# A transfer of later stages' norm weights from GpSimd's queue at the start, and the lambda weights computed in the second pair of chunks

## The chip, the cores and the metric

The kernel runs on one core of a Trainium2 chip. The metric is the device time of one execution in microseconds (us); each run gives one time. The engines are named as in the profile: PE (TensorE's matmuls) and PEld (its weight loads), DVE (VectorE), ACT (ScalarE), POOL (GpSimd), and SP (SyncE, which issues most of the DMAs). A "q" behind a name (SPq) means the engine's instruction queue.

## What is computed

Two layers of a residual trunk over 256 tokens with 2048 columns, all in float32. Each layer has a mixer with two groups of eight heads (stick-breaking attention, and differential attention with a learned lambda) and a SwiGLU stage of width 5632. Cut to the places that matter here:

```python
def reference(x, ...):
    for l in range(DEPTH):                       # 2 layers
        h = rms_norm(x, pre_mix_norm[l])
        m = hybrid_mixer(h, l, ...)
        x = x + rms_norm(m, post_mix_norm[l])
        h = rms_norm(x, pre_ffn_norm[l])
        f = swiglu(h, w_gate[l], w_up[l], w_down[l])
        x = x + rms_norm(f, post_ffn_norm[l])

def hybrid_mixer(h, layer, w_in, w_o, ...):
    proj = h @ w_in                              # 2048 x 6144, q k v of both groups
    ...
    lam = (jnp.exp(jnp.sum(lq1 * lk1)) - jnp.exp(jnp.sum(lq2 * lk2)) + lam_init)
    o_d = differential_attention(q1, q2, k1, k2, v_d, lam)     # softmax1 - lam * softmax2
    o_d = rms_norm(o_d, diff_subln) * (1.0 - lam_init)
    return concat(o_sb, o_d) @ w_o
```

lambda depends on four vectors of 64 numbers for each layer, and on nothing else.

## The kernel before

**Precision by splitting.** Each float32 operand is split into a rounded part hi (made by ACT, line 286) and the rest lo (made by DVE, line 289), and each product is three matmuls: hi with hi (line 1017), hi with lo (1018), lo with hi (1019). All weights are read once from HBM, in one stream of tiles of 128x1024 (512 KB, named raw, GU, G, T or V) whose order `weight_order` fixes. `fetch` issues the loads on SP's queue, `feed` makes hi and lo, four tiles ahead of the product that needs them. There are four raw buffers and six each of hi and lo: a load waits until DVE has split the tile that had its buffer, and a split waits until PE has used up the tile three pairs of rows before.

**The input projection.** 12 chunks of 512 output columns are computed in six pairs (`PAIRS`: first 6 and 8, the rotary q and k of the differential group; then 10 and 7; and so on). For each pair a loop runs over the eight pairs of rows kp. For most kp there are eight products for the two chunks and the two halves of the tokens (`eight_in`, four ticks). From the second pair on, kp 4 and 5 use seven products in place of eight (`seven_in`, `seven_products`). For these, `mixed_weights` (lines 258 to 274) builds sums of weight blocks: DVE adds (264), ACT and DVE split (259, 260), DVE subtracts (267) and adds (268), and the sums are split into Th and Tl (259, 260). Their products go to the banks p and q (p_in, q_in in the profile). After the last seven-product step `shared_part` combines them on DVE (lines 1055 to 1058) into w.

**The opening.** The first pair of layer 0 runs in `opening`, which loads x by columns (xr) and the first weights in small pieces. Beside it `first_stats` loads x by rows (x0) for the norm's sums, and at its last step calls `late_constants`: the rest of the gains (columns 32 to 96: the norm weights of the ffn stage, of layer 1 and of both attention outputs), the rope table, the four lambda vectors broadcast to 128 partitions, some constant matrices made by POOL, and the whole arithmetic of lambda (lines 399 to 413), which ends in `lamsign`. At the start of the kernel POOL also makes the identity (`make_identity`, two instructions listed as masks.py:197 and masks.py:199); a cast of it to bf16 (line 393) runs on DVE in the opening, between the splits.

**After a pair.** `settle` evacuates the banks (tok, line 913, on ACT). For chunks 6 and 8 POOL rotates tok (lines 786 to 789, with the rope table). `flip` transposes them (qkT_ps on PE, qT and kT on ACT, line 932). `diff_weights` then makes the softmax weights and multiplies by `lamsign` (line 749): for the first time at 99.63 us.

**What sets the order.** The engines run their own instruction lists in order. The list is made by a scheduler from the program's order and estimated times. Generators started with `start` are advanced by `tick`, which the product loops call: a value that a generator yields is the number of ticks until its next step. `tc.issue_after(...)` keeps an instruction behind another one: `in_turn` behind the last weight load, `after_rests` behind the last split made on DVE, `not_ahead` behind a load some places earlier. DMAs on SP signal one of eight semaphores in rotation, so a load also waits for the transfer eight places ahead.

**Memory.** `late_constants` takes its temporary tiles from the tag t2 (four buffers, shared with the sums of the seven-product steps). `early_room` hands out four rooms of 128x1024 in rotation: first to the four x0 tiles, later to the outputs of the differential heads, then to the ffn stage.

Of the kernel before, what the change touches and what calls it, by code (L numbers as in the profile page):

```python
# [17 lines left out]
P = 128  # L18
D = 2048
S = 256  # L20
L = 2
# [36 lines left out]
def lambda_init(layer):  # L58
    return 0.8 - 0.6 * math.exp(-0.3 * layer)
# [94 lines left out]
def kernel(  # L154
# [153 lines left out]
    def in_turn():  # L308

        return tc.issue_after(loads[-1].ins)  # L310
# [67 lines left out]
    lamsign = const.tile([P, L, 4], F32, name="lamsign")  # L378

    def late_constants(pool):  # L380
        lams = pool.tile([P, 4, L * 64], F32, tag="t2", name="lams")
        negones = pool.tile([P, P], F32, tag="t2", name="negones")
        nc.sync.dma_start(gains[:, 32:96], gain_columns[:, 32:96])
        nc.sync.dma_start(rope_sb, rope.rearrange("(t p) c -> p t c", p=P))
        for i, v in enumerate((lambda_q1, lambda_k1, lambda_q2, lambda_k2)):
            nc.sync.dma_start(lams[:, i, :], v.rearrange("l d -> (l d)").partition_broadcast(P))
        nc.gpsimd.memset(negones, -1.0)
        nc.vector.tensor_copy(negone, negones)
        nc.gpsimd.affine_select(
            out=negones, in_=negones, compare_op=ALU.is_ge, fill=0.0, base=0, pattern=[[-1, P]], channel_multiplier=1  # L390
        )
        nc.vector.tensor_copy(negtri, negones)
        nc.vector.tensor_copy(ident16, ident)
        nc.gpsimd.memset(hidden, NEG)
        nc.gpsimd.affine_select(
            out=hidden, in_=hidden, compare_op=ALU.is_ge, fill=0.0, base=0, pattern=[[-1, P]], channel_multiplier=1
        )
        nc.gpsimd.memset(lamsign, 1.0)
        lprod = pool.tile([P, 2, L * 64], F32, tag="t2", name="lprod")
        lsum = pool.tile([P, 2, L], F32, tag="t2", name="lsum")  # L400
        for i in range(2):
            nc.vector.tensor_tensor(out=lprod[:, i, :], in0=lams[:, 2 * i, :], in1=lams[:, 2 * i + 1, :], op=ALU.mult)
            nc.vector.tensor_reduce(
                out=lsum[:, i, :], in_=lprod[:, i, :].rearrange("p (l d) -> p l d", l=L), axis=AX.X, op=ALU.add
            )
        nc.scalar.activation(lsum, lsum, AF.Exp)
        for l in range(L):
            c0 = 80 + l * NH
            nc.vector.tensor_scalar_mul(gains[:, c0 : c0 + NH], gains[:, c0 : c0 + NH], 1.0 - lambda_init(l))
            for q in range(2):  # L410
                col = lamsign[:, l, 2 * q + 1 : 2 * q + 2]
                nc.vector.tensor_tensor(out=col, in0=lsum[:, 1, l : l + 1], in1=lsum[:, 0, l : l + 1], op=ALU.subtract)
                nc.vector.tensor_scalar_add(col, col, -lambda_init(l))

    const.tile([P, LEVEL], F32, name="level")
    eps = const.tile([P, 1], F32, name="eps")
# [374 lines left out]
    def opening(pool, accs, xT, stats, sums_of, settle):  # L791

        xr = []

        def load():
            kp = len(xr)
            xr.append(pool.tile([P, 2, S], F32, tag="tok", name=f"xr{kp}"))
            nc.sync.dma_start(xr[kp], x_columns[:, 2 * kp : 2 * kp + 2, :])

        def split(k):  # L800
            g, src = gains[:, k : k + 1], xr[k // 2][:, k % 2, :]
            nc.scalar.activation(xT[k][:, 0, :], src, AF.Copy, scale=g)
            nc.vector.scalar_tensor_tensor(
                out=xT[k][:, 1, :], in0=src, scalar=g, in1=xT[k][:, 0, :].bitcast(F32), op0=ALU.mult, op1=ALU.subtract
            )

        load()
        both = []
        for i in range(2):
            both.append((  # L810
                wpool.tile([P, 2, CW], F32, tag="raw", bufs=4, name=f"raw{i}"),
                wpool.tile([P, 2, CW], F32R, tag="hi", bufs=6, name=f"hi{i}"),
                wpool.tile([P, 2, CW], F32R, tag="lo", bufs=6, name=f"lo{i}"),
            ))
            raws.append(both[i][0])
        for kk in range(2):
            for i in range(2):
                loads.append(nc.sync.dma_start(raws[i][:, kk, :], stream[i][:, kk, :]))
        load()
        fetch(4)  # L820
        for kk in range(2):
            split(kk)
            for raw, hi, lo in both:
                nc.scalar.activation(hi[:, kk, :], raw[:, kk, :], AF.Copy)
                nc.vector.tensor_tensor(out=lo[:, kk, :], in0=raw[:, kk, :], in1=hi[:, kk, :].bitcast(F32), op=ALU.subtract)
        for i in range(2):
            ready[i] = both[i][1:]
        fed[0] = 2
        for kp in range(KT // 2):
            if kp:  # L830
                split(2 * kp)
                split(2 * kp + 1)
            if kp + 2 < KT // 2:
                load()
                fetch(2 * kp + 6)
            for part in ((0,), (1,)) if kp == KT // 2 - 1 else (range(NT),):
                eight_in(accs, xT, 0, PAIRS[0], kp, part, kp == 0, kp == KT // 2 - 1, 0)
                if kp == KT // 2 - 1:
                    settle(part[0])
            if 3 <= kp < 7:  # L840
                next(stats)
            if kp >= 4 and kp - 4 < len(IN_SEVEN):
                sums_of(IN_SEVEN[kp - 4])
# [38 lines left out]
    def mixer_in(pool, l, rs, xT, mix, mixed):  # L882
# [7 lines left out]
        for n, cc in enumerate(PAIRS):  # L890
# [52 lines left out]

            if n == 0 and l == 0:
                opening(pool, banks, xT, first_stats(pool, rs), sums_of, settle)
            else:
                kps = IN_ORDER if n else tuple(range(KT // 2))
                extra = None
                burst[0] = clock[0] + 4 * kps.index(mine[0]) if mine and n else None
                for j, kp in enumerate(kps):  # L950
                    first, last = j == 0, j == len(kps) - 1
                    if n == 0 and 2 <= j < 2 + len(IN_SEVEN):
                        sums_of(IN_SEVEN[j - 2])
                    if n == 0 and 3 <= j < 7:
                        put_away(f"in{l}", j - 3)
                    if kp in mine:
                        if extra is None:
                            assert math.inf not in taken
                            extra = four_banks(True, [f"{q}_in{l}_{n}" for q in ("p1", "p6", "p7", "q5")])
                        seven_in(banks, extra, forms[kp], xT, l, cc, kp, kp == mine[0], kp == mine[-1])  # L960
                        if kp == mine[-1]:
                            burst[:] = None, clock[0] + SETTLE
                            w = pool.tile([P, 4, CW], F32, tag="gpost", bufs=1, name=f"w{l}_{n}")
                            with tc.high_priority(offset=URGENT):
                                shared_part(extra, [w[:, i, :] for i in range(4)])
                            if n + 1 < len(PAIRS) and IN_NOW[n + 1]:
                                burst[0] = clock[0] + 4 * (len(kps) - 1 - j) + 4 * IN_ORDER.index(IN_NOW[n + 1][0])
                            else:
                                pool.end_of_sums()
                                mix_pool[0] = pool  # L970
                        continue
                    if n == 0 and j < 2:
                        if j == 0:
                            for t in range(NT):
                                for kp in kps[:2]:
                                    eight_in(banks, xT, l, cc, kp, (t,), kp == kps[0], False)
                        continue
                    if first or last:
                        for t in range(NT):
                            eight_in(banks, xT, l, cc, kp, (t,), first, last)  # L980
                            if last:
                                settle(t)
                    else:
                        eight_in(banks, xT, l, cc, kp, range(NT), first, last)
                    if j == 0 and n == len(PAIRS) - 1:
                        xs[:] = [[late_room([P, D // 2], f"x{l}_{t}_{h}") for h in range(2)] for t in range(NT)]
                        with in_turn():
                            for t, h in ((0, 0), (0, 1), (1, 0), (1, 1)):
                                load_x(t, h, away[-1] if l else None)
# [387 lines left out]
```

## Time and profile before

| | |
|---|---|
| median of three runs | 2197.44 us (2195.82 to 2197.62) |
| profiled execution | 2197.66 us, span 2196.0 us |
| PE busy in the span | 2177.9 us (99%), 9991 matmuls |
| DVE, ACT, POOL busy | 1902.1 us (87%), 1370.5 us (62%), 138.6 us (6%) |
| HBM read, mean rate | 457.00 MB, 212 GB/s over the span |
| transfers issued by POOL | 110, the first at 417.23 us |
| gains, rope and the lambda loads issued by SP | at 34.16, 34.97, and 36.23 to 38.89 us |
| arithmetic of lambda on DVE | between 43.16 and 48.30 us |

How to read the lines below. A line of a timeline gives the start in us from the span's first instruction, the duration in us, the engine, the line of the kernel, the operation, the tile written and the tiles read, shapes, and how often. In brackets stands the idle time of the engine just before it, and what ended it. A line of the waits gives who waited for whom: us in total, times, longest. A line of the windows gives a stretch and its length, then for PE, PEld, DVE, ACT and POOL the busy time and the number of instructions, then the granted clock of TensorE as a share of full speed, the share of the DMA engines, and GB/s. Matmuls overlap, so the distance between starts tells PE's pace, not the duration of one.

### The profile page before, as it was taken

The numbers are of one execution on the slowest core, as the hardware profiler recorded it, in microseconds if no ns is written. First come the engines' busy times: TensorE is split into PE (matmuls) and PEld (weight loads), VectorE is DVE, ScalarE is ACT, GpSimd is POOL, SyncE is SP. The second block draws the span as 40 slices with busy tenths as digits, with TensorE's granted clock in tenths as the row PEclk, the third lists the DMA queues.
The fourth block names the chain that finished last, engine by engine and source line by source line (L and its number), as shares of the span: only waits on it lengthen the run. The fifth ranks groups of instructions, "written<-read, shape, count | busy, mean of one in ns | idle before, by whom it ended". The sixth has DMA issues, their size and how long they took to land.

```text
span 2196.0 us, 28541 instructions
## 1 busy us (share of the span) xinstructions
PE 2177.9 (99%) x9991; PEld 1790.8 (82%) x9991; DVE 1902.1 (87%) x2609; ACT 1370.5 (62%) x2052; POOL 138.6 (6%) x186
## 2 busy tenths in 40 slices
PE   9999999999999999999999999999999999999998
PEld 7788888788888888888878888888888888888886
DVE  7888658899999999989878886589999999999997
ACT  7566665756656656666665666657665566566664
POOL 1200000000001000000011000000000100100000
PEclk9999999999999999999999999999999999999999
DMA  9555555488687676767465455555867766767673
GB/s 308 200 170 173 192 182 172 155 279 256 196 266 243 197 251 203 244 214 262 151 251 173 160 179 189 192 170 190 276 216 244 258 216 224 241 212 234 206 266 98
DMA packets 138513, 467.28 MB, mean 213 GB/s; under 512 B 15872, under 2 KB 16640, under 8 KB 137856
## 3 DMA queue, kind: packets, MB, share of 16 engines
q1 hardware_dynamic: 122384, 436.59, 57.0%
q0 software_dynamic: 15840, 28.84, 7.5%
q8 instruction: 78, 1.28, 0.2%
q14 instruction: 67, 0.55, 0.1%
q10 hardware_dynamic: 144, 0.02, 0.0%
HBM read 457.00 MB, written 8.39 MB: 212 GB/s over the span
## 4 chain that ended last, share of the span: by engine, by line
PE 90%; DVE 4%; DMA 3%; ACT 2%; issue 1%; DVEq 0%; POOL 0%; ACTq 0%; POOLq 0%; SPq 0%
PE c L1018 9%; PE c L1019 9%; PE c L1017 9%; PE in L1017 6%; PE in L1019 6%; PE in L1018 6%; PE dn L1261 4%; PE dn L1259 4%; PE dn L1258 4%; PE p L1018 2%; PE p L1019 2%; PE p L1017 2%; PE o L528 2%; PE o L529 2%; PE o L530 2%; DMA raw<-in_weights_in_turn_dram 2%
## 5 line engine op out<-in xcount | busy, mean ns | idle before, releaser
L289 DVE TENSOR_TENSOR lo<-raw,hi 128x1024 fp32r<-128x1024 f32 x522 | 625.6, 1219 | 98.0 <-ACT hi L286 97.2
L286 ACT ACTIVATE hi<-raw 128x1024 fp32r<-128x1024 f32 x522 | 540.4, 1055 | 188.0 <-issue 51.8
L1017 PE MATMUL c<-hi,xF 128*128 128x512 f32 x834 | 328.0, 394 | 0.1
L1018 PE MATMUL c<-lo,xF 128*128 128x512 f32 x834 | 325.1, 390 | 0.7 <-DVE lo L289 0.7
L1019 PE MATMUL c<-hi,xF 128*128 128x512 f32 x834 | 324.8, 390 | 0.0
L238 POOL DMA_DIRECT2D T<-in_weights_in_turn_dram x110 | 95.9, 874 | 1684.5 <-DMA T<-in_weights_in_turn_dram 496.5
L1018 PEld LDWEIGHTS c<-lo,xF 128*128 128x128 f32 x834 | 156.7, 188 | 33.5 <-DVE lo L289 2.5
L1019 PEld LDWEIGHTS c<-hi,xF 128*128 128x128 f32 x834 | 156.5, 188 | 32.7
L1017 PEld LDWEIGHTS c<-hi,xF 128*128 128x128 f32 x834 | 156.7, 188 | 31.5 <-ACT xF L447 0.5
L1258 PE MATMUL dn<-hi,jh 128*128 128x512 f32 x432 | 168.3, 389 | 0.0
L1259 PE MATMUL dn<-lo,jh 128*128 128x512 f32 x432 | 168.1, 389 | 0.0
L289 DVE TENSOR_TENSOR lo<-G,hi 128x1024 fp32r<-128x1024 f32 x110 | 133.9, 1218 | 29.8 <-ACT hi L286 29.6
L259 ACT ACTIVATE hi<-T 128x1024 fp32r<-128x1024 f32 x110 | 115.5, 1050 | 45.6 <-PE c L1019 31.3
L259 ACT ACTIVATE Th<-G 128x1024 fp32r<-128x1024 f32 x110 | 116.1, 1055 | 37.9 <-DVE G L268 35.9
L260 DVE TENSOR_TENSOR Tl<-G,Th 128x1024 fp32r<-128x1024 f32 x110 | 133.9, 1217 | 5.3 <-ACT Th L259 5.3
L260 DVE TENSOR_TENSOR lo<-T,hi 128x1024 fp32r<-128x1024 f32 x110 | 133.9, 1217 | 4.3 <-ACT hi L259 4.0
L268 DVE TENSOR_TENSOR G<-G,T 128x1024 f32<-128x1024 f32 x110 | 134.2, 1220 | 2.1
L259 ACT ACTIVATE Th<-T 128x512 fp32r<-128x512 f32 x110 | 68.9, 627 | 104.6 <-DVE T L267 88.7
L1261 PE MATMUL dn<-hi,jl 128*128 128x512 f32 x432 | 132.9, 390 | 0.0
L1017 PE MATMUL in<-hi,xT 128*128 128x512 f32 x328 | 131.3, 401 | 0.0
L1017 PE MATMUL in<-hi,xI 128*128 128x512 f32 x328 | 131.1, 401 | 0.0
L1018 PE MATMUL in<-lo,xT 128*128 128x512 f32 x328 | 128.2, 391 | 0.4 <-DVE lo L289 0.4
(448 smaller groups left out, 4736.8 us busy)
## 6 DMA issues: line engine op xcount, KB each, us to landing
raw<-in_weights_in_turn_dram SPq DMA_DIRECT2D x522, 512.0 KB, 4.5
T<-in_weights_in_turn_dram SPq DMA_DIRECT2D x110, 512.0 KB, 6.3
G<-in_weights_in_turn_dram SPq DMA_DIRECT2D x110, 512.0 KB, 5.8
T<-in_weights_in_turn_dram POOLq DMA_DIRECT2D x110, 256.0 KB, 7.1
GU<-in_weights_in_turn_dram SPq DMA_DIRECT2D x32, 512.0 KB, 6.2
V<-in_weights_in_turn_dram SPq DMA_DIRECT2D x8, 512.0 KB, 4.1
away_ffn<-x SPq DMA_DIRECT2D x8, 512.0 KB, 8.4
xd<-away_ffn SPq DMA_DIRECT2D x8, 512.0 KB, 8.4
```

Of the source, the lines that this page charges most:

```text
L238: nc.gpsimd.dma_start(sums[i][:, 0, :], stream[i - 1][:, 0, :], accum_op=ALU.add)
L259: nc.scalar.activation(h, w, AF.Copy)
L260: nc.vector.tensor_tensor(out=l, in0=w, in1=h.bitcast(F32), op=ALU.subtract)
L268: nc.vector.tensor_tensor(out=g, in0=g, in1=t2.unsqueeze(1).to_broadcast([P, 2, CW]), op=ALU.add)
L286: nc.scalar.activation(hi, raw, AF.Copy)
L289: rest = nc.vector.tensor_tensor(out=lo, in0=raw, in1=hi.bitcast(F32), op=ALU.subtract)
L1017: nc.tensor.matmul(a, sh, hi, start=first, stop=False, skip_group_check=open_sums[0])
L1018: nc.tensor.matmul(a, sh, lo, start=False, stop=False, skip_group_check=open_sums[0])
L1019: nc.tensor.matmul(a, sl, hi, start=False, stop=last, skip_group_check=open_sums[0])
L1258: nc.tensor.matmul(accs[c, t], sh, hi[:, kk, :], start=first, stop=False, skip_group_check=open_sums[0])
L1259: nc.tensor.matmul(accs[c, t], sh, lo[:, kk, :], start=False, stop=False, skip_group_check=open_sums[0])
L1261: nc.tensor.matmul(accs[c, t], sl, hi[:, kk, :], start=False, stop=last, skip_group_check=open_sums[0])
```

## The change

The load of gains 32 to 96 is issued by POOL's queue and no longer by SP's. In the instruction list it stands near the start of POOL's queue, behind the memset of the identity and of eps, ahead of masks.py:199.

The lambda work leaves `late_constants`. A new generator `lambdas` is started when the opening's program has been written out, with its tiles in one early room. Its four loads are issued in turn with the weights; sixteen ticks later come the products, sums, the Exp and the scalings, with the first of them held behind the last split. In the instruction lists the four loads stand on SP behind the sixth weight load of the second pair; the arithmetic stands on DVE behind the two splits of kp 6 of the second pair and among the four instructions of `shared_part`, with the last steps around the two splits of kp 7. Exp stands on ACT between the first and the second copy into qT.

As the scheduler works from estimated times, some neighbours change places too. On DVE the copies negone and negtri stand earlier in the opening. For kp 4 and kp 5 of the second pair, one split of plain weights stands behind the subtraction (267) where it stood ahead of it, or behind the wide Tl where it stood ahead of it. On ACT the splits of the second pair's first four tiles stand partly ahead of the evacuations (tok) of the opening's banks; before, only the first one did. On PE, in both seven-product steps, the three products of p7 with the wide Th and Tl stand together, where other products stood between them. From about the third pair on the lists of all engines are the same.

```diff
--- before.py
+++ after.py
@@ -378,12 +378,9 @@
     lamsign = const.tile([P, L, 4], F32, name="lamsign")
 
     def late_constants(pool):
-        lams = pool.tile([P, 4, L * 64], F32, tag="t2", name="lams")
         negones = pool.tile([P, P], F32, tag="t2", name="negones")
-        nc.sync.dma_start(gains[:, 32:96], gain_columns[:, 32:96])
+        nc.gpsimd.dma_start(gains[:, 32:96], gain_columns[:, 32:96])
         nc.sync.dma_start(rope_sb, rope.rearrange("(t p) c -> p t c", p=P))
-        for i, v in enumerate((lambda_q1, lambda_k1, lambda_q2, lambda_k2)):
-            nc.sync.dma_start(lams[:, i, :], v.rearrange("l d -> (l d)").partition_broadcast(P))
         nc.gpsimd.memset(negones, -1.0)
         nc.vector.tensor_copy(negone, negones)
         nc.gpsimd.affine_select(
@@ -396,21 +393,33 @@
             out=hidden, in_=hidden, compare_op=ALU.is_ge, fill=0.0, base=0, pattern=[[-1, P]], channel_multiplier=1
         )
         nc.gpsimd.memset(lamsign, 1.0)
-        lprod = pool.tile([P, 2, L * 64], F32, tag="t2", name="lprod")
-        lsum = pool.tile([P, 2, L], F32, tag="t2", name="lsum")
+
+    def lambdas():
+
+        room = early_room([P, 2 * CW], "lams")
+        lams = room[:, 0 : 4 * L * 64].rearrange("p (i c) -> p i c", i=4)
+        lprod = room[:, 4 * L * 64 : 6 * L * 64].rearrange("p (i c) -> p i c", i=2)
+        lsum = room[:, 6 * L * 64 : 6 * L * 64 + 2 * L].rearrange("p (i l) -> p i l", i=2)
+        with in_turn():
+            for i, v in enumerate((lambda_q1, lambda_k1, lambda_q2, lambda_k2)):
+                nc.sync.dma_start(lams[:, i, :], v.rearrange("l d -> (l d)").partition_broadcast(P))
+        yield 16
         for i in range(2):
-            nc.vector.tensor_tensor(out=lprod[:, i, :], in0=lams[:, 2 * i, :], in1=lams[:, 2 * i + 1, :], op=ALU.mult)
+            with after_rests():
+                nc.vector.tensor_tensor(out=lprod[:, i, :], in0=lams[:, 2 * i, :], in1=lams[:, 2 * i + 1, :], op=ALU.mult)
             nc.vector.tensor_reduce(
                 out=lsum[:, i, :], in_=lprod[:, i, :].rearrange("p (l d) -> p l d", l=L), axis=AX.X, op=ALU.add
             )
         nc.scalar.activation(lsum, lsum, AF.Exp)
         for l in range(L):
             c0 = 80 + l * NH
-            nc.vector.tensor_scalar_mul(gains[:, c0 : c0 + NH], gains[:, c0 : c0 + NH], 1.0 - lambda_init(l))
+            with after_rests():
+                nc.vector.tensor_scalar_mul(gains[:, c0 : c0 + NH], gains[:, c0 : c0 + NH], 1.0 - lambda_init(l))
             for q in range(2):
                 col = lamsign[:, l, 2 * q + 1 : 2 * q + 2]
                 nc.vector.tensor_tensor(out=col, in0=lsum[:, 1, l : l + 1], in1=lsum[:, 0, l : l + 1], op=ALU.subtract)
                 nc.vector.tensor_scalar_add(col, col, -lambda_init(l))
+        yield
 
     const.tile([P, LEVEL], F32, name="level")
     eps = const.tile([P, 1], F32, name="eps")
@@ -943,6 +952,7 @@
 
             if n == 0 and l == 0:
                 opening(pool, banks, xT, first_stats(pool, rs), sums_of, settle)
+                start(lambdas())
             else:
                 kps = IN_ORDER if n else tuple(range(KT // 2))
                 extra = None
```

## The prediction, made before the changed kernel ran

> **What bounds the kernel.** I read the page's busy table first, then the waits of PE over the whole span, because in a kernel whose PE is busy 99% only those waits can be won back.
>
> ```profile
> PE 2177.9 (99%) x9991; PEld 1790.8 (82%) x9991; DVE 1902.1 (87%) x2609; ACT 1370.5 (62%) x2052; POOL 138.6 (6%) x186
> ```
> ```profile
> PE p L1018 <- DVE Tl L260: 1.8, 3, 0.9
> PE xT_ps L444 <- DVE xd L574: 1.4, 1, 1.4
> PE p L1017 <- ACT Th L259: 1.3, 1, 1.3
> PE p_in L1017 <- ACT Th L259: 1.3, 1, 1.3
> PE spare L367 <- DVE idle L364: 1.3, 1, 1.3
> PE c L1018 <- DVE lo L289: 0.7, 2, 0.4
> PE in L1018 <- DVE lo L289: 0.6, 2, 0.4
> ```
>
> All waits together are 8.4 us. The change touches the first pair of chunks and the second; there lie only the single p_in wait and, in part, the last row. The timeline of PE shows where p_in stands:
>
> ```profile
> 64.14 0.39 PE L1018 MATMUL q_in<-lo,shin 128*128 128x512 f32 x1
> 64.37 0.39 PE L1019 MATMUL q_in<-hi,slin 128*128 128x512 f32 x1
> 66.08 0.73 PE L1017 MATMUL p_in<-Th,shin 128*128 128x512 f32 x2 [1.31 <-ACT Th L259]
> ```
>
> Matmuls start 0.23 us apart (64.14 to 64.37), so the next was due at 64.60 and came at 66.08: 1.48 us lost. That is the prize. It is the first seven-product step (kp 4 of the second pair), which waits for the split Th of the mixed weights. Following Th backwards, in the chain of waits and on the timelines of ACT and DVE:
>
> ```profile
> 39.62 8.28 DMA raw<-in_weights_in_turn_dram
> ```
> ```profile
> 47.32 0.21 ACT L406 ACTIVATE lsum<-lsum 128x4 f32<-128x4 f32 x1 [4.92 <-DVE lsum L403]
> 47.98 1.06 ACT L286 ACTIVATE hi<-raw 128x1024 fp32r<-128x1024 f32 x1 [0.46 <-DMA raw<-in_weights_in_turn_dram]
> ```
> ```profile
> 51.98 1.26 ACT L913 ACTIVATE tok<-in,rs_in 128x512 f32<-128x512 f32 x2
> 53.12 1.07 ACT L286 ACTIVATE hi<-raw 128x1024 fp32r<-128x1024 f32 x1
> 54.07 1.07 ACT L286 ACTIVATE hi<-GU 128x1024 fp32r<-128x1024 f32 x1
> ```
> ```profile
> 55.41 1.34 DVE L289 TENSOR_TENSOR lo<-GU,hi 128x1024 fp32r<-128x1024 f32 x1
> 56.68 0.95 DVE L264 TENSOR_TENSOR GU<-GU,GU 128x512 f32<-128x512 f32 x1
> 58.75 1.37 DVE L260 TENSOR_TENSOR lo<-GU,hi 128x1024 fp32r<-128x1024 f32 x1 [1.13 <-ACT hi L259]
> 60.05 1.48 DVE L289 TENSOR_TENSOR lo<-raw,hi 128x1024 fp32r<-128x1024 f32 x1
> 61.45 0.81 DVE L267 TENSOR_TENSOR GU<-GU 128x512 f32<-128x512 f32 x1
> 62.19 1.34 DVE L289 TENSOR_TENSOR lo<-raw,hi 128x1024 fp32r<-128x1024 f32 x1
> 63.45 1.48 DVE L268 TENSOR_TENSOR GU<-GU,GU 128x1024 f32<-128x1024 f32 x1
> 64.86 0.68 DVE L260 TENSOR_TENSOR Tl<-GU,Th 128x512 fp32r<-128x512 f32 x1
> 65.46 1.21 DVE L289 TENSOR_TENSOR lo<-GU,hi 128x1024 fp32r<-128x1024 f32 x1
> 66.59 1.21 DVE L260 TENSOR_TENSOR Tl<-GU,Th 128x1024 fp32r<-128x1024 f32 x1
> ```
>
> The reader should see two idle stretches of ACT: 4.92 us for the lambda sums, 0.46 us for weights whose first load started only at 39.62, behind gains, rope and four lambda loads on SP, and landed 8.28 us later.
>
> **Part 1, five loads leave SP's queue ahead of the weights.** In the changed order SP has only rope between the last x load and the first raw of the second pair. That raw can go once its buffer is free. ACT stood idle from 42.40 (47.32 - 4.92), and it no longer has Exp ahead of the weights; the loads need to land only some 2.1 us sooner for two hi of 1.06 to be done before the tok copies, and five issues fewer ahead of them give that (an estimate; if not, it is the first rival). What is late next is PE: the two tok copies at 51.98 evacuate the last opening banks and stay where they are. In the changed order all four raw splits stand before them, so the hi that began at 53.12 is gone from there and hi<-GU begins at 53.12 instead of 54.07 and ends at 54.19. DVE then starts lo<-GU near 54.3, 1.1 us earlier than 55.41.
>
> **Part 2, the order on DVE.** The order in which the two programs issue differs here in one helpful place: the lo of 60.05 stands behind L267 instead of ahead of it. L267 therefore moves by 1.1 and by 1.4 more (60.05 to 61.45), to 58.95. One lo still lies between L267 and L268, as before, so L268 starts 2.0 later, at 60.95. Th came 1.52 after the start of L268 and took 1.06:
>
> ```profile
> 64.97 1.06 ACT L259 ACTIVATE Th<-GU 128x1024 fp32r<-128x1024 f32 x1 [1.09 <-DVE GU L268]
> ```
>
> So Th is ready near 63.5, 1.1 us before 64.60: the 1.48 us goes. But PE's order changes too. Before, PE ran the second use of Th and other products ahead of the first Tl of the wide half; now Th, Tl, Th stand together, so Tl<-GU 128x1024 is wanted at 64.83. On DVE it comes behind L268, the narrow Tl and one lo: 60.95 + 1.41 + 0.60 + 1.13 = 64.1 at the uncontended spacing, 64.25 if the lo is slowed like the one at 62.19; plus 1.21 gives 65.3 to 65.5. A new wait of 0.5 to 0.65 us takes part of the prize. I take 0.6; the ends are 0 (slowing gone) and 1.5 (nothing won).
>
> [...] Slowed and unslowed rows of the same POOL line:
>
> ```profile
> 50.59 0.31 POOL L787 TENSOR_TENSOR rb<-tok,rope_sb 128x64 f32<-128x64 f32 x1
> ```
> ```profile
> 60.40 1.31 POOL L787 TENSOR_TENSOR rb<-tok,rope_sb 128x64 f32<-128x64 f32 x1
> ```
>
> The rotations last at least until 61.7 and DVE's 128x1024 subtractions take 1.34 to 1.48 beside them against 1.21 alone. The rotations start from tok copies that PE paces, so I leave them in place. [...]
>
> **Part 3, the lambda work in the second pair.** Loads: four, behind the second GU load; their landing is not wanted until DVE comes to them near 78. Work on DVE, by the groups of that window:
>
> ```profile
> L402 DVE TENSOR_TENSOR lprod<-lams 128x128 f32<-128x128 f32 x2 | 0.6, 293 | 3.0 <-DMA lams<-in_lambda_k_dram 2.9
> L403 DVE TENSOR_REDUCE lsum<-lprod 128x2 f32<-128x128 f32 x2 | 0.6, 286 | 0.1
> ```
> ```profile
> L412 DVE TENSOR_TENSOR lamsign<-lsum 128x1 f32<-128x1 f32 x4 | 0.4, 154 | 0.3 <-ACT lsum L406 0.3
> ```
>
> With four more column steps and two scalings of gains, taken at the 154 ns of the last row, that is 0.6 + 0.6 + 10 x 0.154 = 2.7 us, set among the four combinations of the shared products, after all weights of kp 5, 3 and 6 are split. Queued behind them on DVE are the two splits of kp 7, then those of the next pair. The cover is DVE's own idle there:
>
> ```profile
> 86.81 2.36 DVE L289 TENSOR_TENSOR lo<-raw,hi 128x1024 fp32r<-128x1024 f32 x2 [3.24 <-ACT hi L286]
> ```
>
> 3.24 us hold 2.7, so I cost it at nothing; without that cover it would cost at most 2.7. Exp on ACT now waits for DVE between two copies of transposed q, with the second qT and two kT copies and the next hi queued behind it; it takes 0.21 and PE has the whole of kp 6 and 7 before it needs that hi. Nothing.
>
> **Part 4, the gains transfer on POOL.** It stands on POOL between two memsets and the select that finishes the identity. Its price there, from the only transfers that POOL issues before (the view of line 238), and the one reader that could be held:
>
> ```profile
> L238 POOL DMA_DIRECT2D T<-in_weights_in_turn_dram x110: 853/866/1218, 417.2 to 2132.5; - x110
> ```
> ```profile
> 1.22 0.29 POOL masks.py:199 TENSOR_SCALAR_AFFINE_SELECT ident<-ident 128x128 f32<-128x128 f32 x1
> ```
> ```profile
> 11.12 0.22 DVE L393 CAST ident<-ident 128x128 bf16<-128x128 f32 x1
> 12.18 2.52 DVE L289 TENSOR_TENSOR lo<-raw,hi 128x1024 fp32r<-128x1024 f32 x2 [0.83 <-ACT hi L286]
> ```
>
> 0.87 to 1.22 us moves the identity from 1.51 to 2.7 at worst; the cast reads it at 11.12. Hidden. Its 32 KB now fall among the first weights. The 512 KB load above took 8.28 us in a full queue; 32 KB at that pace are 0.5 us, at the other end is nothing. I charge 0.1, nearer to nothing, because the first loads are issued before it.
>
> **Sum.** -1.48 + 0.6 + 0.1 = -0.8 us. The profiled execution took 2197.66 (span 2196.0 and 1.7 around it), the median is 2197.44; I subtract from the median: 2196.6. From about 100 us on, the order on every engine is the same in both programs, so the rest shifts as a block. A change below 0.2% (4.4 us) is about what a measurement of this kernel can't tell from none.
>
> **Rivals.**
> - *The new wait takes all of it.* Tl's wait of 0.6 grows to 1.5 if the loads land as late as before (47.9): 2197.5. For: DVE's rows from 60.05 to 66.59 show no idle before them, so each slip is passed on. Against: ACT's 4.92 idle is gone. 18%.
> - *The clock.* Where PE was busy for only 3.78 of 6 us, the granted clock fell to 0.79:
>
> ```profile
> 430.00:436.00 6.00, 3.78 (x11) 2.67 (x11) 6.00 (x12) 4.53 (x5) 0.00 (x0) 0.79 0.00 0
> ```
>
> 0.21 of 6 us is 1.3 us. A shift by about 1 us can make it vanish (2195.3, with the whole prize 2194.6) or give another gap one of its own (2197.9, without the prize 2198.7). [...] 8%.
> - *The first POOL transfer is slow, and the kernel slower.* The identity's select is behind it, the cast behind that on DVE, and all weight splits behind the cast. It decides from 11.12 - 1.51 = 9.6 us, and with DVE's idle of 0.83 from 10.4; each us beyond it is a us of PE. A hold of 16 us gives 2197.4 - 0.8 + 5.6 = 2202.2. For: no POOL transfer before 417 is in the trace. Against: the longest of 110 is 1.22. [...] 10%, with which I count any other unforeseen wait of that size.
> - *Faster by over 4.4 us.* It would need more than half of all waits of PE, most of them in stages whose order doesn't change. 4%.
>
> **Numbers.** The forecast has 60%. The range 2194.0 to 2199.5 takes in the first two rivals with the clock either way and the spread of the three times (1.8 us); it leaves out the last two. Faster by over 0.2% 0.04, slower 0.10, within 0.86.
>
> **What would show it.** Right: the p_in wait on Th missing, one on Tl of 0.3 to 0.9 in its place near 65; first raw load of the second pair issued before 37; hi<-GU starting at 53.1; no new wait of PE between 75 and 100; POOL's transfer below 1.5 us and the cast near 11.1. Wrong: Th still waited for, DVE late on kp 7 near 88, or a gap of PE before 14.

## The result and the profile after

The changed kernel takes 2192.31 us (median of 14 runs, 2191.73 to 2193.77), the kernel before 2197.72 us in the same comparison (14 runs, 2195.46 to 2200.58). The ratio is 0.9975, with a 95% interval of 0.9968 to 0.9983: 5.4 us faster, where 0.8 was forecast. The profiled execution took 2192.54 us, with a span of 2190.8.

The busy table and the waits of PE, as for the kernel before (lines of the program from about 400 on now bear numbers higher by 9 or 10, so L1027, L1028 and L1029 are the three products):

```profile
PE 2175.4 (99%) x9991; PEld 1789.5 (82%) x9991; DVE 1901.4 (87%) x2609; ACT 1370.4 (63%) x2052; POOL 141.0 (6%) x187
```
```profile
PE xT_ps L453 <- DVE xd L583: 1.4, 1, 1.4
PE spare L367 <- DVE idle L364: 1.3, 1, 1.3
PE p L1028 <- DVE Tl L260: 0.8, 2, 0.5
PE c L1028 <- DVE lo L289: 0.7, 2, 0.4
PE in L1027 <- ACT xT L811: 0.6, 1, 0.6
PE in L1028 <- DVE lo L289: 0.5, 2, 0.3
PE p L1027 <- ACT Th L259: 0.4, 1, 0.4
```

The wait of p_in for Th (1.3) is gone, as forecast. But two more rows of the old table shrank that the forecast left alone: p on Tl from 1.8 to 0.8, p on Th from 1.3 to 0.4. These are banks of the ffn stage, not of the input projection. By the timelines the 1.3 on Th at 431.45 us and the 0.9 on Tl at 432.84 are gone altogether; the 0.4 on Th in this table is another wait, at 1560.62 us. (The new row of 0.6 on xT lies in the opening, at 6.88 us.) What happened there is seen when the same matmuls are put side by side. Timeline of PE, kernel before:

```profile
429.73 0.39 PE L1019 MATMUL q<-hi,sl 128*128 128x512 f32 x1
431.45 0.50 PE L1017 MATMUL p<-Th,sh 128*128 128x512 f32 x1 [1.33 <-ACT Th L259]
432.84 0.50 PE L1018 MATMUL p<-Tl,sh 128*128 128x512 f32 x1 [0.88 <-DVE Tl L260]
...
435.08 0.63 PE L1018 MATMUL c<-lo,sh 128*128 128x512 f32 x1
435.51 0.63 PE L1019 MATMUL c<-hi,sl 128*128 128x512 f32 x1
...
437.05 0.39 PE L1017 MATMUL p<-hi,xF 128*128 128x512 f32 x1
```

And the changed kernel:

```profile
428.47 0.39 PE L1029 MATMUL q<-hi,sl 128*128 128x512 f32 x1
428.70 0.39 PE L1027 MATMUL p<-Th,sh 128*128 128x512 f32 x1
428.93 0.39 PE L1028 MATMUL p<-Tl,sh 128*128 128x512 f32 x1
...
431.42 0.39 PE L1027 MATMUL p<-hi,xF 128*128 128x512 f32 x1
```

Up to q<-hi,sl the changed kernel is 1.26 us ahead (429.73 - 428.47), at p<-hi,xF it is 5.63 ahead (437.05 - 431.42). So 4.4 us of the gain lie in one place of some 8 us, the first seven-product step of the ffn stage of layer 0, some 340 us behind the last instruction that the change moves. Two things make up the 4.4. Two waits: from 429.73 to 432.84 PE takes two steps in 3.11 us in place of 0.46, a loss of 2.7. And the clock: at 435.08 to 435.51 matmuls start 0.43 us apart, not 0.23. The windows of both kernels (after the length: PE, PEld, DVE, ACT, POOL busy, then the granted clock), before and then after:

```profile
432.00:438.00 6.00, 5.16 (x16) 4.08 (x17) 6.00 (x9) 4.52 (x7) 0.00 (x0) 0.72 0.00 0
```
```profile
432.00:438.00 6.00, 6.00 (x29) 4.95 (x28) 6.00 (x7) 3.17 (x5) 0.00 (x0) 1.00 0.68 230
```

A clock of 0.72 over 6 us is 1.7 us lost. Together 2.7 + 1.7 = 4.4. The rest of the 5.1 between the two profiled executions (2197.66 - 2192.54) is the lead of 1.26 us that stood ahead of this place, most of it the 1.48 at 64 us that the forecast named, less small new waits (below), and later shifts: some 0.4 us gained near 479 us and some 1 us lost between 1549 and 1568 us.

**Why the stage was late before.** The answer stood in the chain of waits of the kernel before, for 405 to 437 us, a view that the prediction did not use:

```profile
407.92 4.35 DMA T<-in_weights_in_turn_dram
412.27 0.03 issue
412.30 0.04 POOLq L238
412.34 4.88 issue
417.22 0.04 POOLq L238
417.26 0.68 POOL T L238
417.94 8.77 DMA T<-in_weights_in_turn_dram
...
426.87 1.06 ACT hi L259
...
429.17 1.14 DVE G L268
```

Line 238 is the transfer with which GpSimd adds one weight tile to another in T. The load that it waits for lands at 412.27 and its semaphore is taken at 412.30. Then comes "issue": 4.88 us in which GpSimd's queue waits for nothing that the profile shows. Only then does the sum go out, and hi of T, G, Th and Tl are late with it. In the changed kernel there is no such stretch. The view of line 238 between 409 and 419 us, before and after:

```profile
L238 POOLq EVENT_SEMAPHORE  x2: 43/43/43, 412.3 to 417.2; - x2
L238 POOL DMA_DIRECT2D T<-in_weights_in_turn_dram x2: 1023/1120/1218, 417.2 to 417.9; - x2
```
```profile
L238 POOLq EVENT_SEMAPHORE  x2: 43/43/43, 411.0 to 414.3; - x2
L238 POOL DMA_DIRECT2D T<-in_weights_in_turn_dram x2: 867/879/891, 411.6 to 414.8; - x2
```

The first sum goes out 0.6 us after its release (411.0 to 411.6) instead of 4.9.

One more thing moved. Queue q14 is listed as "instruction"; by that name I take its transfers for ones that bring instructions, not data. In the DMA views of 411 to 418 us before and of 145 to 153 us after stands the same row, and in the other stretch of each kernel there is none:

```profile
q14 instruction: 1, 0.01, 0.3%
```

q14's transfers come all along the run (67 in the kernel before), and the view doesn't say for which engine. That this one is GpSimd's is inferred: between 100 and 460 us both kernels have twelve, and the others come at like times in both (none over 8 us apart).

### The profile page after: what moved, and what is told of

Its sections match the earlier page's. It is cut to its first block, busy times and chain, and to the rows that moved or that the text cites. A ratio compares the mean times of both kernels' runs of the same rounds, so it can differ in the third digit from the quotient of the medians.

```text
span 2190.8 us, 28542 instructions
## 1 busy us (share of the span) xinstructions
PE 2175.4 (99%) x9991; PEld 1789.5 (82%) x9991; DVE 1901.4 (87%) x2609; ACT 1370.4 (63%) x2052; POOL 141.0 (6%) x187
## 4 chain that ended last, share of the span: by engine, by line
PE 92%; DVE 4%; ACT 2%; DMA 1%; issue 1%; SPq 0%; DVEq 0%; ACTq 0%
PE c L1028 9%; PE c L1029 9%; PE c L1027 9%; PE in L1027 7%; PE in L1029 7%; PE in L1028 7%; PE dn L1271 4%; PE dn L1269 4%; PE dn L1268 4%; PE p L1028 2%; PE p L1029 2%; PE p L1027 2%; PE o L537 2%; PE o L538 2%; PE o L539 2%; DVE lo L289 1%
## 5 line engine op out<-in xcount | busy, mean ns | idle before, releaser
L1027 PE MATMUL c<-hi,xF 128*128 128x512 f32 x834 | 328.1, 394 | 0.1
L1028 PE MATMUL c<-lo,xF 128*128 128x512 f32 x834 | 325.2, 390 | 0.7 <-DVE lo L289 0.7
L1029 PE MATMUL c<-hi,xF 128*128 128x512 f32 x834 | 324.8, 390 | 0.0
L1028 PEld LDWEIGHTS c<-lo,xF 128*128 128x128 f32 x834 | 156.7, 188 | 33.8 <-DVE lo L289 2.8
L1029 PEld LDWEIGHTS c<-hi,xF 128*128 128x128 f32 x834 | 156.5, 188 | 32.8
L1027 PEld LDWEIGHTS c<-hi,xF 128*128 128x128 f32 x834 | 156.6, 188 | 31.5 <-ACT xF L456 0.5
L1027 PE MATMUL in<-hi,xT 128*128 128x512 f32 x328 | 131.3, 401 | 0.6 <-ACT xT L811 0.6
L1027 PE MATMUL in<-hi,xI 128*128 128x512 f32 x328 | 131.1, 401 | 0.0
L1028 PE MATMUL in<-lo,xT 128*128 128x512 f32 x328 | 128.2, 391 | 0.3 <-DVE lo L289 0.3
```

Source lines behind the costliest of these rows:

```text
L1027: nc.tensor.matmul(a, sh, hi, start=first, stop=False, skip_group_check=open_sums[0])
L1028: nc.tensor.matmul(a, sh, lo, start=False, stop=False, skip_group_check=open_sums[0])
L1029: nc.tensor.matmul(a, sl, hi, start=False, stop=last, skip_group_check=open_sums[0])
```

## Experiments

Three theories of this stop of 4.88 us were set against each other. *Refill* supposes that GpSimd's instructions come in blocks, that the next block is fetched when its list reaches a certain place, and that before the change this place fell between the release and the issue of the first T sum, where the q14 row lies; any instruction more or less on GpSimd's list would move it away. *Cold* supposes that the first transfer that GpSimd issues is slow, and that the gains transfer takes that on itself in the opening. *Shift*: an accident of timing, which the 1.5 us gained ahead, or any disturbance, cures.

**1. The lambda work alone (a1_lambda_only).** The changed kernel with gains back on SP:

```diff
-        nc.gpsimd.dma_start(gains[:, 32:96], gain_columns[:, 32:96])
+        nc.sync.dma_start(gains[:, 32:96], gain_columns[:, 32:96])
```

> The changed kernel with the gains load back on SP's queue, so that only the lambda work is moved; POOL issues nothing new. [...] Shift theory (the stop is an accident of timing that 1.5 us less ahead of it cure): 2192.3.

Measured: 2192.07 us, ratio 0.997 (0.9959 to 0.998). No stop: the first sum goes out at 411.78, 0.65 us after its release. By Refill and by Cold the stop was to stay and only the 1.5 us at 64 us to be won, 2197.7 - 1.5 = 2196.2; only Shift's 2192.3 came true.

Cold falls here: no GpSimd transfer stands ahead of this one. Refill's number was missed as well, because I had taken GpSimd's list to be as long as before. It isn't: with the lambda work moved, the scheduler's other order of copies and splits leaves one more wait among GpSimd's instructions, of the kind that stands there as an instruction of its own (EVENT_SEMAPHORE in the view of line 238, two of 43 ns beside the two transfers). The first T sum has 66 ahead of it, where it had 65 (counted in the two programs' lists).

**2. The gains transfer alone (a2_gains_only).** The kernel before with only the diff's line for gains.

> The kernel before with only the gains load moved to POOL; the lambda work stays in the opening. Refill theory and cold theory: no stop of POOL ahead of the first T sum, so the stalls of PE near 430 (1.5 + 1.2 us) and the half clock behind them (2.2) go: 2197.7 - 4.3 to 4.9 = 2192.8 to 2193.4 us; the wait on Th near 64 stays. Shift theory: 2197.6.

Measured: 2193.43 us, ratio 0.9979 (0.9971 to 0.9988). The sum goes out at 412.13, without a stop. PE still waits for Th at 65 us (0.8 us), so the gain at 64 us isn't needed for it: Shift's form in which that gain is the cure falls.

**3. No transfer, no lambda, two memsets (a3_two_memsets).** The kernel before, and nothing but:

```diff
-    nc.gpsimd.memset(eps, EPS)
+    for _ in range(3):
+        nc.gpsimd.memset(eps, EPS)
```

> The kernel before with two more memsets of eps on POOL in the opening, and no transfer by POOL there. Refill theory: two instructions more are enough, the stop moves into the rotations near 150 and the stalls near 430 go: 2192.8 to 2193.4 us. Cold theory: the first transfer is still the first T sum, the stop stays, 2197.7. Shift theory: 2197.7.

Measured: 2193.34 us, ratio 0.9977 (0.9968 to 0.9986). Two useless memsets of 0.1 us in the opening win as much as the transfer of gains.

**4. The changed kernel with two memsets fewer (a4_after_two_fewer).** The memsets of hidden and lamsign are given to DVE.

> The changed kernel, with its early transfer on POOL, but with two memsets (hidden and lamsign) made by DVE, so that POOL's list is two instructions shorter and counts as the one before up to the first T sum. Refill theory: the stop of about 5 us ahead of the first or the second T sum is back, with the stalls near 430: 2196.2 us. Cold theory: the early transfer has paid, no stop, 2192.3. Shift theory: 2192.3.

Measured: 2192.00 us, ratio 0.9972 (0.9961 to 0.9983); the sum goes out at 411.33. Refill as I had worded it was wrong again: two instructions fewer don't bring the stop back. The q14 transfer is back between 411 and 419 us, but no stop is with it. So a q14 transfer there is not yet a stop; the exact place must matter. The next four runs move it one at a time.

**5. The lambda work alone, with one instruction fewer (b1_lambda_one_fewer).** Against experiment 1:

```diff
-        nc.gpsimd.memset(lamsign, 1.0)
+        nc.vector.memset(lamsign, 1.0)
```

> The kernel of the lambda-only experiment with its ones for lamsign written by DVE: one GpSimd instruction fewer, so that the first T sum stands as far down GpSimd's list as in the kernel before (slot 65 of the program order, against 66), while the 1.5 us gained at 64 us stay. Refill (the stop belongs to the place in GpSimd's list): GpSimd stops again for some 5 us between the release of the first T sum near 411 us and its issue, an instruction fetch lies near 414 and not near 149, TensorE waits at 423 to 428 us and its clock falls: the time goes back up by the 4.2 us that the stop was worth, 2192.1 to about 2196.3. Shift (the stop needs the exact timing of the kernel before, or any edit ahead cures it): no stop, 2192.1.

Measured: 2196.99 us, ratio 0.9995 (0.9986 to 1.0004), 4.9 us above experiment 1 by the medians. (Experiments 1 to 4 and 5 to 8 were timed in two comparisons; the kernel before had 2198.16 us in the first and 2197.45 in the second.) The stop is back, by the chain of waits of this kernel:

```profile
411.52 0.04 POOLq L238
411.57 4.80 issue
416.37 0.04 POOLq L238
```

So are PE's waits and the slow clock:

```profile
428.87 0.39 PE L1029 MATMUL q<-hi,sl 128*128 128x512 f32 x1
430.79 0.51 PE L1027 MATMUL p<-Th,sh 128*128 128x512 f32 x1 [1.53 <-ACT Th L259]
432.18 0.79 PE L1028 MATMUL p<-Tl,sh 128*128 128x512 f32 x1 [0.88 <-DVE Tl L260]
```
```profile
430.00:436.00 6.00, 4.33 (x11) 3.25 (x12) 6.00 (x12) 4.29 (x6) 0.00 (x0) 0.72 0.00 0
```

A memset of 0.1 us, moved from one engine to another, costs some 4.9 us. This run decides for the place in the list: the gain at 64 us is there, the order around the stage is that of the changed kernel, and the stop comes back when the number ahead of the first T sum is 65 again.

**6. The kernel before with one instruction fewer (b2_before_one_fewer).** The same one-line edit, on the kernel before.

> The kernel before with lamsign's ones written by DVE: the first T sum one slot higher in GpSimd's list (64). Refill, with the refill asked for one instruction later: the first T sum goes out about 0.6 to 0.9 us after its release as in the run with two memsets fewer, and the stop falls on the second T sum or on nothing: 2193.4 if on nothing, up to 2198 if the second sum is as late as before. Shift: 2193.4 by accident or 2198 if this edit is too small to move anything.

Measured: 2193.79 us, ratio 0.998 (0.9971 to 0.9988). The same edit that costs 4.9 us in experiment 5 gains 3.7 here. Both sums go out:

```profile
411.76 1.02 POOL L238 DMA_DIRECT2D T<-in_weights_in_turn_dram  x1 [260.83 <-PE c L1018]
413.93 0.87 POOL L238 DMA_DIRECT2D T<-in_weights_in_turn_dram  x1 [1.14 <-DMA T<-in_weights_in_turn_dram]
440.96 0.86 POOL L238 DMA_DIRECT2D T<-in_weights_in_turn_dram  x1 [26.16 <-DMA T<-in_weights_in_turn_dram]
```

The q14 transfer is still between 411 and 419 us, at 415.43. It falls into the 26 us in which GpSimd waits for its next load anyway; that it costs nothing for that reason is an inference.

**7. The kernel before with one memset of eps more (b3_before_one_more).** As experiment 3, with range(2).

> The kernel before with one more memset of eps on GpSimd: slot 66. Refill: the fetch moves from 415 to about 150 us, where GpSimd has nothing to do for 260 us, no stop, 2193.3 as with two more. Shift or any theory in which the number of GpSimd instructions has no part: the memset of some 0.1 us in the opening moves nothing, the stop stays, 2197.7.

Measured: 2193.65 us, ratio 0.9982 (0.9973 to 0.9991). The sum goes out at 412.13, and the q14 transfer is between 145 and 153 us, beside the last rotations on GpSimd, which run on without a stop; a pause of GpSimd of 260 us follows.

**8. The kernel before with two instructions fewer (b4_before_two_fewer).** lamsign and hidden are filled by DVE.

> The kernel before with lamsign's ones and hidden's fill written by DVE: slot 63. Refill: the refill is asked for two instructions later than in the kernel before, after the first T sum has gone out: the stop falls on the second T sum (then between 2193.4 and 2198, by how late it is) or behind both (2193.4). No part for the count: 2197.7.

Measured: 2193.19 us, ratio 0.9979 (0.997 to 0.9988). Sums at 412.73 and 415.48, no stop.

The runs without a GpSimd transfer in the opening, by the number of instructions ahead of the first T sum:

| ahead | kernel | first T sum released, issued | q14 transfer | us |
|---|---|---|---|---|
| 63 | before, two fewer | 412.1, 412.7 | 411 to 419 | 2193.19 |
| 64 | before, one fewer | 411.1, 411.8 | 411 to 419 | 2193.79 |
| **65** | **before** | **412.3, 417.2** | 411 to 418 | **2197.45** |
| **65** | **lambda alone, one fewer** | **411.5, 416.4** | 411 to 418 | **2196.99** |
| 66 | before, one more | 411.5, 412.1 | 145 to 153 | 2193.65 |
| 66 | lambda alone | 411.1, 411.8 | 145 to 153 | 2192.07 |
| 67 | before, two more | 411.7, 412.3 | 145 to 153 | 2193.34 |

The stop is one place wide. It is there at 65, with or without the lambda change, and at no other number from 63 to 67. It isn't the time of the release: 411.5 us comes with the stop (lambda alone, one fewer) and without it (before, one more). And it carries the whole gain at that place: from q<-hi,sl to the p<-hi,xF shown above PE takes 7.32 us in the kernel before and 7.50 in experiment 5, and 2.95 in every version without the stop, experiments 2 and 4 and the changed kernel among them. That the place in GpSimd's list makes the stop, and that it costs some 4 to 5 us (4.4 between these two matmuls, 3.7 to 4.9 by the medians), is shown for kernels without a GpSimd transfer in the opening.

That the engine waits for the fetch is an inference, a close one: q14's transfer lies beside the stop in both kernels that have it, and one instruction more moves both away. In both it starts 3.0 us behind the release (415.33, 414.52) and takes 0.3 us. Two things stay open. Why the stop lasts 4.9 us was not tried. And experiment 4 doesn't fit the count: up to the release its trace has 68 records of GpSimd, as many as both kernels with the stop (the table's 64 has 67, its 66 has 69), but no stop, and its fetch lies where 63 and 64 have it. With a GpSimd transfer in the opening the count is off by at least one.

All versions without the stop and with the lambda work moved lie at 2192.0 to 2192.3 us, and those with it in the opening at 2193.2 to 2193.8. Within experiments 1 to 4 the lambda move is worth 1.3 to 1.4 us; with the stop in both kernels (experiment 5 against the kernel before) the difference of 0.5 us is within the interval. By the traces PE gains 1.1 us on the kernel before between 64 and 100 us in all four versions that have it, and 0.0 to 0.4 in the others. None of these versions is faster than the changed kernel by more than the intervals.

## Why the prediction was wrong

**Part 1 held**, and came out a little larger. The first four weight loads of the second pair are issued from 35.02 us, and hi<-GU begins at 52.53, forecast 53.12:

```profile
35.02 6.51 SPq L220 DMA_DIRECT2D raw<-in_weights_in_turn_dram  x4
```
```profile
52.53 1.07 ACT L286 ACTIVATE hi<-GU 128x1024 fp32r<-128x1024 f32 x1
```

**Part 2 held in its mechanism; the new wait was mis-sized.** The steps came in the order forecast, each some 0.5 to 0.7 us ahead of its number:

```profile
58.28 0.84 DVE L267 TENSOR_TENSOR GU<-GU 128x512 f32<-128x512 f32 x1
59.04 1.34 DVE L289 TENSOR_TENSOR lo<-raw,hi 128x1024 fp32r<-128x1024 f32 x1
60.30 1.34 DVE L268 TENSOR_TENSOR GU<-GU,GU 128x1024 f32<-128x1024 f32 x1
...
63.57 1.21 DVE L260 TENSOR_TENSOR Tl<-GU,Th 128x1024 fp32r<-128x1024 f32 x1
```
```profile
64.23 0.39 PE L1029 MATMUL q_in<-hi,slin 128*128 128x512 f32 x1
64.46 0.39 PE L1027 MATMUL p_in<-Th,shin 128*128 128x512 f32 x1
64.84 0.50 PE L1028 MATMUL p_in<-Tl,shin 128*128 128x512 f32 x1
```

Th is there in time (0.23 behind the matmul ahead of it), so the prize of 1.48 was paid. Tl ends at 64.78 in place of 65.3 to 65.5, and the wait for it is 0.38 - 0.23 = 0.15 us, not 0.6. Most of it is early because the evacuations (tok) ahead of hi<-GU, forecast to stay at 51.98, began at 51.39. The forecast left out that kp 5 has the same order of products on PE, and so a wait for Tl of its own, of 0.48 - 0.23 = 0.25 us:

```profile
74.95 0.39 PE L1027 MATMUL p_in<-Th,shin 128*128 128x512 f32 x1
75.43 0.50 PE L1028 MATMUL p_in<-Tl,shin 128*128 128x512 f32 x1
```

So the second pair gave 1.48 - 0.15 - 0.25 = 1.1 us, near the forecast's 1.48 - 0.6 = 0.9, and that nearness is luck: a wait taken too large stood in for one left out.

**Part 3 held.** The arithmetic stands on DVE from 77.67 to 83.73 us, the idle stretch ahead of the splits of kp 7 shrinks from 3.24 to 1.70, and no wait of PE follows: between 10 and 135 us the list of PE's waits has one row only, 0.3 us on a lo, at 13.51 us in the opening.

```profile
85.58 2.36 DVE L289 TENSOR_TENSOR lo<-raw,hi 128x1024 fp32r<-128x1024 f32 x2 [1.70 <-ACT hi L286]
```

**Part 4 was right on the duration and blind to the count.** The transfer takes 0.71 us, the identity's select follows at 2.21, and the cast comes at 11.22 (11.12 before):

```profile
1.42 0.71 POOL L382 DMA_DIRECT2D gains<-in_gain_columns_dram  x1 [0.36 <-issue]
2.21 0.32 POOL masks.py:199 TENSOR_SCALAR_AFFINE_SELECT ident<-ident 128x128 f32<-128x128 f32 x1
```

The select starts 0.1 us behind the transfer's end, so the rival of a slow first transfer has nothing in the trace, and experiments 1 and 3 refute Cold, the other form of it. The 0.1 us charged for its 32 KB can't be read from the runs: at 50 us their traces lie from 0.62 us behind the kernel before to 0.56 ahead of it, in no order of the edits. What I left out is that an instruction more on a list moves everything behind it by a place.

**The sum failed at one sentence**: "From about 100 us on, the order on every engine is the same in both programs, so the rest shifts as a block." The order is the same. The place of each instruction in GpSimd's list is not, and the first T sum stood on the one place with a stop of 4.88 us. What the sum put at nothing behind 100 us measured 4.4 us at this place alone. The row for it was in the prediction: "417.2 to 2132.5" gives the start of the first T sum, and I used it only for the durations 853/866/1218. The two waits of PE that it makes, p on Th (1.3) and on Tl (0.9), stood in the first table quoted; I set them aside as lying outside the stages that the change touches and never followed them back. The chain of waits of that window shows 4.88 us of "issue" on GpSimd, and the change puts an instruction on GpSimd's list.

**The rivals.** The clock was the right one to suspect at that place, with the wrong mechanism and price. It was costed as a stretch that a shift of 1 us may move (1.3 us, from 0.79 in 430 to 436). That was an estimate of mine, and no run shows it: experiment 5 comes to q<-hi,sl 0.86 us ahead of the kernel before (428.87 against 429.73) and is granted the same 0.72 from 432 to 438 us. In these runs the slow clock comes with the two waits: from 432 to 438 us it was 0.72 in both kernels that have the stop and 1.00 in the eight others. The price of the pair is 2.7 + 1.7 = 4.4 us; the window from 430 had cut the slow stretch short. In windows of 1 us the kernel before was granted 0.71, 0.50, 0.50 and 0.58 from 433 to 437 us, and 1.00 in those on either side: again 1.7 us lost, or 3.4 us at 0.50. Two waits of together 2.65 us, one matmul apart, were enough; how short a wait would still bring it was not shown. The case "faster by over 4.4 us" was said to need more than half of all waits of PE. That sum counts waits only; at the clock of 0.50 PE was busy all the time (1.00 of each us from 433 to 437), so the 1.7 us stood in no row of waits, and the bound was too tight.

## What to carry to other kernels

When an edit adds or removes instructions on an engine, ask where that engine's list stalls without a cause ("issue" in the chain of waits, or a stretch between a release and the next start that is far longer than its neighbours), because one instruction can move such a stall away or call it up hundreds of us later (here a memset made in the first 3 us, and a stop near 412). Before a difference of some 0.2% is credited to what an edit means, run a twin that only changes the count (a useless memset): here two of them alone won 4.8 us (2198.16 to 2193.34), where the whole change won 5.4. And follow the largest waits back even in stages that the edit does not touch; those rows are the list of what can change by accident.

## What the runs showed that was not expected

- GpSimd's queue stops for 4.88 us (4.80 in experiment 5) between a release and the next instruction when the first T sum has 65 instructions ahead of it, and for about 0.6 us at 63, 64, 66 and 67 (kernels without a GpSimd transfer in the opening). A q14 transfer lies beside the stop (415.33 and 414.52 us).
- No stop is seen where the q14 transfer comes shortly ahead of a pause of the engine: 260 us behind the rotations at 145 to 152 us, or 26 us behind the second T sum.
- Two waits of PE of 1.72 - 0.23 and 1.39 - 0.23 us, one matmul apart, were followed by 3.4 us at a granted clock of 0.50. A single one of like size at 64.37 us in the kernel before, 1.48 us, was not: matmuls there go on 0.23 apart, and the clock from 64 to 70 us is 1.00.
